# The MLP's first product as seven quadrant products, in two passes over its weights

## The chip, the core and the metric

The kernel runs on one core of a Trainium2 chip. The metric is device microseconds of one execution. Engines: PE (TensorE, matmuls and transposes), DVE (VectorE), ACT (ScalarE), POOL (GpSimd), and SP, whose queue issues nearly all DMAs.

## The reference

Two transformer blocks run one after the other on 1024 tokens of 1024 channels, in float32. The change touches only the last part of the second block, a squared-ReLU MLP with 4096 hidden channels:

```python
def sqrelu_mlp(h, ln_g, w1, w2):
    u = rmsnorm_2(h, ln_g) @ w1          # [1024, 1024] @ [1024, 4096]
    return jnp.square(jax.nn.relu(u)) @ w2   # [1024, 4096] @ [4096, 1024]

def second_block(x, ...):
    h = x
    h = h + hybrid_mixer(h, ...)         # ends in a product with w_out
    h = h + sqrelu_mlp(h, ln_ff_g, w_ff1, w_ff2)
    return rmsnorm_2(h, ln_final_g)
```

## The kernel before

The program is recorded first and then put in order: every engine call goes through `Program.record` (line 346 issues nearly all instructions, so the profile's lines say L346 throughout), each gets a cost from a price table, and `flush` picks on each engine the ready operation of highest priority (the longest chain behind it). The result is a fixed order for each of the five queues; each engine then works through its row in order and waits by semaphores. SBUF is two areas, one for float32 tiles (`sbuf_61` in the order's rows) and one for tiles that PE reads (`sbuf_62`). Addresses are reused: a tile that is laid over a freed one waits for the last use of the old one.

Float32 products are made of three matmuls. Each operand is split into a high half (rounded by an ACT copy) and a low half (DVE: operand minus high half), and `mm3` adds hi x hi, hi x lo and lo x hi in PSUM. One matmul is 128 x 128 x 512.

The part around the change, in program order:

- `mixer2` ends with the out-projection. In two column halves of 512, for each of eight row tiles of 128 tokens, `tok_block` makes 24 matmuls (8 channel blocks x 3), and `ev_o` adds the result on DVE to the residual `xres[tt]`, which is loaded from `hb_d`. A row tile is final after its part in the second column half.
- `mlp` norms each row tile (`normed_T`): the sum of squares on ACT, two small operations on POOL, the scaling on DVE, then eight PE transposes into two PSUM banks, evacuated by ACT (high half) and DVE (low half) into `h`, which overlays `self.y`, the input of the out-projection.
- Then 16 rounds `e` of 256 hidden channels. `chan_block` makes 128 hidden channels for the 1024 tokens: 2 token halves x 8 channel blocks x 3 matmuls, weights as the stationary operand; ACT takes the ReLU and its square (high half), DVE the low half. Then the second product for these 256 hidden channels: 2 column halves x 8 row tiles x 2 x 3 matmuls, each group of six added by DVE to `xres[tt]`. So every row tile is updated in every round and becomes final in the last one.
- Weights come by SP in pieces of 512 KB into a ring `wraw`, and are split into slots `whi`, `wlo`.
- At the end each row tile is normed (ACT, two on POOL, DVE) and stored.

Of the kernel before, what the change touches and what calls it, by code (L numbers as in the profile page):

```python
# [561 lines left out]
class Kern:  # L562
# [1471 lines left out]

    def normed_T(self, pn, x, row, h, tt):
        r = self.sumsq(pn, x, 'nt')
# [263 lines left out]
                                  sr.rearrange("p h e -> p (h e)"))  # L2300


    def mlp(self):
# [4 lines left out]
        with ExitStack() as cn:
            pn = self.pool('pn2', ctx=cn)
            row = self.bcast_row(ins['ln_ff_g_2'][0], D, 'row', pn)  # L2310
            for tt in range(NT):
                self.normed_T(pn, self.xres[tt], row, h, tt)
        for tag in ('whi', 'wlo'):
            self.wp.trim(tag, 3)
        self.nw = 3
        with ExitStack() as cu:
            pu = self.pool('pu', ctx=cu)
            for e in range(16):
                uh, ul = [self.t(pu, [128, 2, T], F32R, tag=n) for n in ('uh', 'ul')]
                for m in range(2):  # L2320
                    def ev_u(half, tok, p):
                        t = self.t(pu, [128, 512], tag='ut', bufs=2)
                        nc.scalar.activation(t, p, AF.Relu)
                        nc.scalar.activation(uh[:, m, tok], t, AF.Square)
                        V.tensor_tensor(out=t, in0=t, in1=t, op=OP.mult)
                        V.tensor_tensor(out=ul[:, m, tok], in0=t, in1=uh[:, m, tok], op=OP.subtract)
                    self.chan_block(w1, 256 * e + 128 * m, 128, h, ev_u)
                for cb in range(2):
                    cs = slice(512 * cb, 512 * cb + 512)
                    wh, wl = self.wload(w2, 256 * e, 512 * cb, 2, 512)  # L2330
                    for tt in range(NT):
                        ts = slice(tt * 128, tt * 128 + 128)
                        p = self.ps([128, 512], 'acc')
                        for k in range(2):
                            self.mm3(p, uh[:, k, ts], ul[:, k, ts], wh[:, k], wl[:, k], k == 0, k == 1)
                        V.tensor_tensor(out=self.xres[tt][:, cs], in0=self.xres[tt][:, cs], in1=p, op=OP.add)
        self.cy.close()
        with ExitStack() as cf:
            pf = self.pool('pf2', ctx=cf)
            row = self.bcast_row(ins['ln_final_g_2'], D, 'row', pf)  # L2340
            for tt in range(NT):
                xt = self.xres[tt]
# [24 lines left out]
```

## Time and profile before

| | |
|---|---|
| median of three runs | 2778.71 us (2775.88 to 2780.1) |
| the profiled execution | 2776.61 us, its span 2774.8 us |
| mean granted TensorE clock | 0.981 |
| busy over the span | PE 94%, DVE 61%, ACT 40%, POOL 22% |
| out-projection's last column half, MLP and end | about 2017 us to 2774.8 us |
| DMA over the span | 468.83 MB, mean 169 GB/s |

A time is given from the start of the span. Busy time of PE counts pipelined matmuls; the granted clock of 1.00 is 2.4 GHz, 0.50 is 1.2 GHz. A row "x3077 | 693.63" means that many instructions in so much busy time; behind a group, the idle time of its engine ahead of it and what ended that.

### The profile page before, as it was taken

Reading aid. Unit: us, or ns where it says so; the run is one execution under the profiler, and the core shown is the slowest. Engines: PE = TensorE matmul, PEld = TensorE weight load, DVE = VectorE, ACT = ScalarE, POOL = GpSimd, SP = SyncE. Lnnn points to the kernel's source line nnn. Section 1 sums busy time; section 2 is a strip of 40 time slices with the busy share of each in tenths; the row PEclk is TensorE's granted clock in tenths of the full one; section 3 lists DMA queues with packets and bytes.
Section 4 is the critical chain, followed back from the end, with each engine's and each line's share of the span. In section 5 each row is a group of like instructions: output and inputs, shape, how many; then the busy total and the mean of one; then the engine's idle time right before and its main releaser. Section 6 shows DMA issues by size and latency. Waiting matters only on the chain. (4 is left out here: it accounts for less than half of the span.)

```text
span 2774.8 us, 35356 instructions
## 1 busy us (share of the span) xinstructions
PE 2609.8 (94%) x12662; PEld 1995.2 (72%) x12662; DVE 1680.3 (61%) x2585; ACT 1104.0 (40%) x1935; POOL 602.2 (22%) x651
## 2 busy tenths in 40 slices
PE   5999999989869999999969999999999999999998
PEld 4787778977657765553526777777888888888886
DVE  8567865556789898676855433377345444444445
ACT  5334332332247676555635432377232212212122
POOL 3016532323431112222234111343100000000001
PEclk9999999999979999999989999999999999999999
DMA  7248586474369999989976423443211111111111
GB/s 248 80 130 239 185 246 178 149 259 153 130 233 352 343 352 333 361 317 359 323 264 218 120 92 105 140 119 82 88 46 47 53 46 54 42 50 54 46 54 68
DMA packets 315792, 468.83 MB, mean 169 GB/s; under 512 B 70170, under 2 KB 140494, under 8 KB 312542
## 3 DMA queue, kind: packets, MB, share of 16 engines
q1 hardware_dynamic: 308958, 449.76, 48.9%
q0 software_dynamic: 6656, 16.79, 1.8%
q8 instruction: 100, 1.64, 0.2%
q14 instruction: 78, 0.64, 0.1%
HBM read 395.62 MB, written 76.76 MB: 170 GB/s over the span
## 5 line engine op out<-in xcount | busy, mean ns | idle before, releaser
L346 PE MATMUL psum_all<-sbuf 128*128 128x512 f32 (+7 forms) x12662 | 2609.8, 367 | 152.5 <-DVE sbuf L346 100.8
L346 PEld LDWEIGHTS psum_all<-sbuf 128*128 128x128 f32 (+4 forms) x12662 | 1995.2, 176 | 766.6 <-issue 159.6
L346 ACT ACTIVATE sbuf<-sbuf 128x1024 fp32r<-128x1024 f32 (+9 forms) x792 | 707.6, 914 | 759.7 <-PE psum_all L346 509.2
L346 DVE TENSOR_TENSOR sbuf<-sbuf,sbuf 128x1024 fp32r<-128x1024 f32 (+3 forms) x538 | 621.1, 1175 | 253.1 <-ACT sbuf L346 246.4
L346 ACT ACTIVATE sbuf<-psum_all 128x512 f32<-128x512 f32 (+14 forms) x774 | 364.2, 481 | 855.8 <-PE psum_all L346 801.1
L346 POOL TENSOR_TENSOR sbuf<-sbuf 128x512 f32<-128x512 f32 (+9 forms) x301 | 361.5, 1209 | 507.6 <-DVE sbuf L346 342.8
L346 DVE TENSOR_TENSOR sbuf<-sbuf 128x512 f32<-128x512 f32 (+16 forms) x345 | 212.0, 628 | 205.3 <-ACT sbuf L346 168.7
L346 DVE TENSOR_TENSOR sbuf<-sbuf,psum_all 128x512 f32<-128x512 f32 (+3 forms) x327 | 217.3, 672 | 161.4 <-PE psum_all L346 161.1
L346 POOL TENSOR_SCALAR sbuf<-sbuf 128x1 f32<-128x1 f32 (+3 forms) x182 | 77.5, 427 | 1031.4 <-ACT sbuf L346 928.7
L346 DVE TENSOR_TENSOR sbuf<-psum_all,sbuf 128x512 f32<-128x512 f32 (+12 forms) x306 | 182.1, 607 | 161.3 <-ACT sbuf L346 82.3
L346 DVE SCALAR_TENSOR_TENSOR sbuf<-sbuf 128x512 f32<-128x512 f32 (+5 forms) x247 | 198.6, 810 | 46.8 <-POOL sbuf L346 36.4
L346 DVE TENSOR_SCALAR sbuf<-sbuf 128x32 f32<-128x32 f32 (+7 forms) x220 | 109.3, 509 | 62.2 <-ACT sbuf L346 42.9
L1808 POOL DMA_INDIRECT y_d<-sbuf x35 | 57.4, 1641 | 195.6 <-DVE sbuf L346 194.4
L346 DVE SCALAR_TENSOR_TENSOR sbuf<-sbuf,psum_all 128x128 f32<-128x128 f32 (+1 forms) x100 | 38.2, 410 | 86.7 <-PE psum_all L346 55.9
L1796 POOL DMA_INDIRECT sbuf<-h_d,sbuf x35 | 44.6, 1273 | 187.0 <-PE psum_all L346 154.0
L346 DVE SCALAR_TENSOR_TENSOR sbuf<-psum_all,sbuf 128x128 f32<-128x128 f32 (+9 forms) x109 | 62.0, 586 | 38.1 <-PE psum_all L346 37.6
L346 DVE CUSTOM_DVE_ANT_0 sbuf<-psum_all,sbuf 128x512 f32<-128x512 f32 (+2 forms) x80 | 48.1, 613 | 23.3 <-PE psum_all L346 22.7
L346 POOL MEMSET sbuf<- 64x64 f32 (+10 forms) x54 | 16.9, 313 | 194.7 <-DVE sbuf L346 114.1
L346 POOL TENSOR_TENSOR sbuf<-sbuf,sbuf 128x1024 fp32r<-128x1024 f32 x16 | 41.1, 2570 | 40.2 <-ACT sbuf L346 39.5
L346 ACT ACTIVATE sbuf<-psum_all,sbuf 128x128 f32<-128x128 f32 (+1 forms) x72 | 24.4, 403 | 35.4 <-PE psum_all L346 22.9
L346 ACT ACTIVATION_READ_ACCUMULATOR sbuf<-sbuf 128x1 f32 x152 | 28.9, 190 | 0.0
L346 DVE COPY sbuf<-psum_all 128x512 f32<-128x512 f32 (+9 forms) x31 | 15.1, 488 | 22.2 <-PE psum_all L346 18.8
(18 smaller groups left out, 112.2 us busy)
## 6 DMA issues: line engine op xcount, KB each, us to landing
sbuf<-in_w SPq DMA_DIRECT2D x384, 512.0 KB
sbuf<-in_w_ff SPq DMA_DIRECT2D x64, 512.0 KB
sbuf<-in_w_in SPq DMA_DIRECT2D x56, 512.0 KB
sbuf<-in_w_ada SPq DMA_DIRECT2D x48, 512.0 KB
sbuf<-in_x SPq DMA_DIRECT2D x16, 512.0 KB
sbuf<-qkv_d SPq DMA_DIRECT2D x32, 256.0 KB
pre_d<-sbuf SPq DMA_DIRECT2D x8, 1024.0 KB
sbuf<-pre_d SPq DMA_DIRECT2D x8, 1024.0 KB
```

The costliest lines, as they stand in the source:

```text
L346: op = self.new_op(eng, lambda: real(*a, **k), name, reads, writes)
L1796: return self.prog.real.gpsimd.indirect_dma_start(out=xg, out_offset=None, in_=self.h2_d, in_offset=bass.IndirectOffsetOnAxis(ap=tok, axis=0),
L1808: st = self.prog.real.gpsimd.indirect_dma_start(out=self.y_d, out_offset=bass.IndirectOffsetOnAxis(ap=dest, axis=0), in_=y, in_offset=None ...
```

## The change

The product u = n @ w1 is made transposed, as w1^T n^T, and cut in 2 x 2 quadrants: A by 512 hidden and 512 input channels within a column group of 1024 hidden channels (four groups `g`), B (`b11`, `b21`, `b12`, `b22`) by 512 input channels and 512 tokens. Winograd's form of Strassen's algorithm makes the four quadrants of u from seven products of quadrants, P1 to P7, in place of eight:

- P1 = A11 B11, P2 = A12 B21, P7 = (A11 - A21) x b7, P6 = S2 x b6 with S2 = A22 - A11 + A21, P5 = (A11 + S2) x b5, P3 = (A12 - S2) x b3, P4 = A22 x b4; b3 is B22 itself, and b4 to b7 are sums and differences of the B quadrants.

Pass 1 makes P1, P2, P7 and P6 for all four groups. P1 + P2 is a quadrant of u and is stored to `u_d`; P1 + P6 and P1 + P6 + P7 are stored to `k_d`, and S2 to `s_d`. Pass 2 loads these and weights again and makes P5, P3 and P4, with the other three quadrants of u stored to `u_d`. Four split B quadrants fit on chip at a time. Then the second product loads u back in units of 256 hidden channels, squares and splits it, and accumulates 512 hidden channels in PSUM (12 matmuls) before DVE adds to the residual. The residual goes to `x_d` and back. Token halves are the outer loop of the second product within 512 hidden channels. The pool of mixer 2 (`c0`) is released ahead of the out-projection instead of behind it.

```diff
@@ mixer2
+        c0.close()
         self.banks = {'acc': (0, 1, 2, 3), 'tp': (4, 5), 'sm': (6, 7)}
...
         for tt in range(NT):
             self.tap('hm', self.xres[tt], slice(tt * 128, tt * 128 + 128))
-        c0.close()
@@ new helpers
+    def halved(self, x, hi=None, lo=None):
...
+        nc.scalar.activation(hi, x, AF.Copy)
+        nc.vector.tensor_tensor(out=lo, in0=x, in1=hi, op=OP.subtract)
+        return hi, lo
+    def quad_product(self, n, A, B, evac):
+        ops = [self.halved(a) for a in A]
+        self.nprod += 1
+        ps = [self.prog.psum_tile([128, 512], 'quad', (4 * (self.nprod % 2) + t,)) for t in range(4)]
+        first = None
+        for j, (ah, al) in enumerate(ops):
+            for t, p in enumerate(ps):
+                m = slice(128 * t, 128 * t + 128)
+                for k in range(2):
+                    bh, bl = [b[:, 2 * j + k] for b in B]
+                    for i, (x, y) in enumerate(((ah, bh), (ah, bl), (al, bh))):
+                        op = nc.tensor.matmul(p, x[:, k, m], y, start=j + k + i == 0, stop=j + k + i == 4)
+                        first = first or op
+                        op.head = first
+        for t, p in enumerate(ps):
+            evac(n, t, p)
@@ mlp, the norm
+                V.scalar_tensor_tensor(t, x, r, row, op0=OP.mult, op1=OP.mult)
+                for k in range(2):
+                    p = self.ps([128, 4, 128], 'tp')
+                    for i in range(4):
+                        nc.tensor.transpose(p[:, i, :], t[:, 512 * k + 128 * i:512 * k + 128 * i + 128], self.ident)
+                    b = q[f'b{k + 1}{tt // 4 + 1}'][:, :, 128 * (tt % 4):128 * (tt % 4) + 128]
+                    if k:
+                        V.tensor_copy(b, p)
+                    else:
+                        nc.scalar.activation(b, p, AF.Copy)
+                nc.sync.dma_start(x_d[tt * 128:tt * 128 + 128], x)
@@ mlp, pass 1
+        b1, b2 = bsplit('b11', 0), bsplit('b21', 1)
+        both(V, 'b12', 'b22', 'b12', OP.subtract)
+        b7 = bsplit('b12', 2)
+        both(V, 'b12', 'b11', 'b12', OP.add)
+        b6 = bsplit('b12', 3)
+        both(G, 'b11', 'b22', 'b12', OP.subtract)
+        both(G, 'b21', 'b21', 'b12', OP.subtract)
+        for g in range(4):
+            a11, a12, a21, a22 = wq(g, 0, 0), wq(g, 0, 1), wq(g, 1, 0), wq(g, 1, 1)
+            def ev(n, t, p):
+                u, v = keep[0][t], keep[1][t]
+                if n in (1, 7):
+                    nc.scalar.activation(u if n == 1 else v, p, AF.Copy)
+                elif n == 2:
+                    out(g, 0, 0, t, u, p)
+                else:
+                    V.tensor_tensor(out=u, in0=u, in1=p, op=OP.add)
+                    V.tensor_tensor(out=v, in0=u, in1=v, op=OP.add)
+                    for i, x in enumerate((u, v)):
+                        nc.sync.dma_start(k_d[128 * g:128 * g + 128, 2048 * i + 512 * t:2048 * i + 512 * t + 512], x)
+            self.quad_product(1, a11, b1, ev)
+            for x, y in zip(a11, a21):
+                V.tensor_tensor(out=y, in0=x, in1=y, op=OP.subtract)
+            self.quad_product(2, a12, b2, ev)
+            self.quad_product(7, a21, b7, ev)
+            for j, (x, y) in enumerate(zip(a22, a21)):
+                V.tensor_tensor(out=y, in0=x, in1=y, op=OP.subtract)
+                nc.sync.dma_start(s_d[128 * g:128 * g + 128, 1024 * j:1024 * j + 1024], y.rearrange("p a n -> p (a n)"))
+            self.quad_product(6, a21, b6, ev)
@@ mlp, pass 2
+        b5, b3, b4 = bsplit('b11', 0), bsplit('b22', 1), bsplit('b21', 2)
+        for g in range(4):
...
+            for t in range(4):
+                for i in range(2):
+                    nc.sync.dma_start(keep[i][t], k_d[128 * g:128 * g + 128,
+                                                      2048 * i + 512 * t:2048 * i + 512 * t + 512])
+            def ev(n, t, p):
+                u, v = keep[0][t], keep[1][t]
+                if n == 5:
+                    out(g, 1, 1, t, v, p)
+                    V.tensor_tensor(out=u, in0=u, in1=p, op=OP.add)
+                elif n == 3:
+                    out(g, 0, 1, t, u, p)
+                else:
+                    out(g, 1, 0, t, v, p)
...
+            self.quad_product(5, a11, b5, ev)
...
+            self.quad_product(3, a12, b3, ev)
+            self.quad_product(4, a22, b4, ev)
@@ mlp, second product
+        for g in range(8):
+            def act(j, th):
+                a = self.t(pa, [128, 2, 512], tag='u', bufs=6)
+                r = ((2 * g + j) * 2 + th) * 128
+                nc.sync.dma_start(a, u_d[r:r + 128].rearrange("p (a n) -> p a n", a=2))
+                V.scalar_tensor_tensor(a, a, 0.0, a, op0=OP.max, op1=OP.mult)
+                return self.halved(a)
+            for th in range(2):
+                A = [act(j, th) for j in range(2)]
+                for cb in range(2):
...
+                        for j in range(2):
+                            for k in range(2):
+                                (ah, al), (wh, wl) = A[j], W[cb][j]
+                                self.mm3(p, ah[:, k, m], al[:, k, m], wh[:, k], wl[:, k], j + k == 0, j + k == 2)
+                        x = xres[4 * th + t][:, cs_]
+                        V.tensor_tensor(out=x, in0=x, in1=p, op=OP.add)
```

`out` adds two tiles on DVE and stores the sum to `u_d`; `bsplit` is `halved` of a B quadrant in two halves; `both` is one operation on a B quadrant in two halves of 128x1024, on DVE (`V`) or POOL (`G`); `wq` loads a weight quadrant in two pieces of 512 KB.

The instructions' order, at three places. First PE's row from the last row tiles of the out-projection on. A MATMUL of 128x128 is a transpose here, one of 128x512 belongs to a product. Before:

```order
L346 MATMUL psum_all<-sbuf_62 128x512 x24
L346 MATMUL psum_all<-sbuf_61 128x128 x8
L346 MATMUL psum_all<-sbuf_62 128x512 x24
L346 MATMUL psum_all<-sbuf_61 128x128 x8
L346 MATMUL psum_all<-sbuf_62 128x512 x24
L346 MATMUL psum_all<-sbuf_61 128x128 x8
L346 MATMUL psum_all<-sbuf_62 128x512 x2
L346 MATMUL psum_all<-sbuf_61 128x128 x8
L346 MATMUL psum_all<-sbuf_62 128x512 x10
L346 MATMUL psum_all<-sbuf_61 128x128 x4
L346 MATMUL psum_all<-sbuf_62 128x512 x6
L346 MATMUL psum_all<-sbuf_61 128x128 x4
```

After, from the same place:

```order
L347 MATMUL psum_all<-sbuf_62 128x512 x156
L347 MATMUL psum_all<-sbuf_61 128x128
L347 MATMUL psum_all<-sbuf_62 128x512 x24
L347 MATMUL psum_all<-sbuf_61 128x128 x7
L347 MATMUL psum_all<-sbuf_62 128x512 x5
L347 MATMUL psum_all<-sbuf_61 128x128
L347 MATMUL psum_all<-sbuf_62 128x512 x19
L347 MATMUL psum_all<-sbuf_61 128x128 x31
L347 MATMUL psum_all<-sbuf_62 128x512 x6
L347 MATMUL psum_all<-sbuf_61 128x128 x24
L347 MATMUL psum_all<-sbuf_62 128x512 x2874
```

The transposes stood in eights between products; now 55 of the 64 stand in two blocks with six product matmuls between (four of P1, two of P2), ahead of the other 2874.

Second, DVE's row at the same place, from the adds of row tiles 2 to 6 on (COPY evacuates four transposes, SCALAR_TENSOR_TENSOR norms a row tile, a `sbuf_62` result is a low half). Before, where these adds stand apart:

```order
L346 TENSOR_TENSOR sbuf_61<-sbuf_61,psum_all 128x512
L346 SCALAR_TENSOR_TENSOR sbuf_61<-sbuf_61 128x1024
L346 TENSOR_TENSOR sbuf_61<-sbuf_61,psum_all 128x512 x3
L346 TENSOR_TENSOR sbuf_62<-psum_all,sbuf_62 128x4x128
L346 TENSOR_TENSOR sbuf_61<-sbuf_61,psum_all 128x512
L346 SCALAR_TENSOR_TENSOR sbuf_61<-sbuf_61 128x1024
L346 TENSOR_TENSOR sbuf_62<-psum_all,sbuf_62 128x512
L346 TENSOR_TENSOR sbuf_62<-psum_all,sbuf_62 128x4x128
L346 TENSOR_TENSOR sbuf_61<-sbuf_61,psum_all 128x512
L346 SCALAR_TENSOR_TENSOR sbuf_61<-sbuf_61 128x1024
L346 TENSOR_TENSOR sbuf_62<-psum_all,sbuf_62 128x512
L346 TENSOR_TENSOR sbuf_62<-psum_all,sbuf_62 128x4x128
```

After:

```order
L347 TENSOR_TENSOR sbuf_61<-sbuf_61,psum_all 128x512 x5
L347 COPY sbuf_61<-psum_all 128x4x128
L347 SCALAR_TENSOR_TENSOR sbuf_61<-sbuf_61 128x1024
L347 TENSOR_TENSOR sbuf_62<-sbuf_61,sbuf_62 128x1024 x3
L347 COPY sbuf_61<-psum_all 128x4x128
L347 SCALAR_TENSOR_TENSOR sbuf_61<-sbuf_61 128x1024
L347 COPY sbuf_61<-psum_all 128x4x128
L347 SCALAR_TENSOR_TENSOR sbuf_61<-sbuf_61 128x1024
L347 COPY sbuf_61<-psum_all 128x4x128
L347 SCALAR_TENSOR_TENSOR sbuf_61<-sbuf_61 128x1024
L347 TENSOR_TENSOR sbuf_61<-sbuf_61,psum_all 128x512
L347 COPY sbuf_61<-psum_all 128x4x128
```

The low half of the transposed tile, a 128x512 subtraction from PSUM, is now a copy, and the normalisations and copies have moved behind the add of row tile 6.

Third, SP's row where pass 1 goes over into pass 2 (before, this queue held only `in_w_ff` loads here):

```order
L347 DMA sbuf_61<-in_w_ff_2 128x2x512
L347 DMA sbuf_61<-k_d 128x512
L347 DMA k_d<-sbuf_61 128x512
L347 DMA sbuf_61<-k_d 128x512
L347 DMA sbuf_61<-x_d 128x1024
L347 DMA sbuf_61<-k_d 128x512
L347 DMA sbuf_61<-in_w_ff_2 128x2x512
L347 DMA sbuf_61<-k_d 128x512
L347 DMA sbuf_61<-s_d 128x1024
L347 DMA u_d<-sbuf_61 128x512
L347 DMA sbuf_61<-k_d 128x512
L347 DMA sbuf_61<-in_w_ff_2 128x2x512
```

Loads of kept sums from `k_d` stand behind their stores, with weight loads, `s_d` and `x_d` loads and the `u_d` stores of P5 between.

## Rows read from the trace of the kernel before

**Rows 1.** The cores' view: span and mean granted clock.

```profile
core 0: 2774.8 us, clock 0.981
```

**Rows 2.** Groups by shape, 2000 to 2775 us: count, busy, mean ns, idle.

```profile
L346 PE MATMUL psum_all<-sbuf 128*128 128x128 f32 x68 | 9.7, 274 | 0.1
L346 DVE TENSOR_TENSOR sbuf<-sbuf,psum_all 128x512 f32<-128x512 f32 x267 | 179.9, 683 | 110.1 <-PE psum_all L346 110.1
L346 DVE TENSOR_TENSOR sbuf<-sbuf,sbuf 128x1024 fp32r<-128x1024 f32 x67 | 82.0, 1223 | 145.1 <-ACT sbuf L346 144.8
L346 ACT ACTIVATE sbuf<-sbuf 128x1024 fp32r<-128x1024 f32 x67 | 71.1, 1061 | 371.6 <-PE psum_all L346 371.0
L346 ACT ACTIVATE sbuf<-psum_all 128x512 f32<-128x512 f32 x64 | 37.6, 588 | 174.0 <-PE psum_all L346 173.9
L346 DVE SCALAR_TENSOR_TENSOR sbuf<-sbuf 128x1024 f32<-128x1024 f32 x16 | 20.4, 1282 | 6.5 <-POOL sbuf L346 5.6 <-PE psum_all L346 0.6
```

**Rows 3.** MLP stretch: sum, busy (count) PE, PEld, DVE, ACT, POOL; clock; DMA.

```profile
2061.89:2755.52 693.63, 693.63 (x3077) 574.46 (x3078) 329.74 (x455) 146.74 (x204) 2.06 (x6) 1.00 0.15 47
```

**Rows 4.** Waits of PE, 2000 to 2775 us: total us, times, longest.

```profile
PE psum_all L346 <- ACT sbuf L346: 1.2, 1, 1.2
```

**Rows 5.** PE in order of time, hand-over: start us, us; in brackets idle before.

```profile
2016.81 43.02 PE L346 MATMUL psum_all<-sbuf 128*128 128x512 f32 x203
2061.07 44.12 PE L346 MATMUL psum_all<-sbuf 128*128 128x512 f32 x209 [1.25 <-ACT sbuf L346]
```

**Rows 6.** PE in order of time and stretches of 2 us around 1815 us.

```profile
1815.74 8.45 PE L346 MATMUL psum_all<-sbuf 128*128 128x288 f32 x40 [2.15 <-DVE sbuf L346]
...
1816.00:1818.00 2.00, 2.00 (x9) 1.98 (x10) 2.00 (x9) 0.91 (x3) 0.57 (x2) 0.50 0.79 255
1818.00:1820.00 2.00, 2.00 (x8) 1.50 (x7) 1.15 (x4) 1.31 (x3) 0.81 (x3) 0.50 0.28 68
1820.00:1822.00 2.00, 2.00 (x12) 1.72 (x12) 1.16 (x5) 1.35 (x3) 1.60 (x2) 0.75 0.31 70
```

**Rows 7.** The end: instructions in order of time; in brackets idle before.

```profile
2755.54 0.69 DVE L346 TENSOR_TENSOR sbuf<-sbuf,psum_all 128x512 f32<-128x512 f32 x1 [0.24 <-PE psum_all L346]
...
2756.32 1.06 ACT L346 ACTIVATE sbuf<-sbuf 128x1024 bf16<-128x1024 f32 x1 [1.55 <-DVE sbuf L346]
...
2757.83 0.55 POOL L346 TENSOR_TENSOR sbuf<-sbuf 128x1 f32<-128x1 f32 x1
...
2758.86 1.28 DVE L346 SCALAR_TENSOR_TENSOR sbuf<-sbuf 128x1024 f32<-128x1024 f32 x1
...
2768.18 1.29 DVE L346 SCALAR_TENSOR_TENSOR sbuf<-sbuf 128x1024 f32<-128x1024 f32 x1 [0.72 <-POOL sbuf L346]
```

**Rows 8.** Stretches by DMA share and GB/s (last two columns), and an array's transfers.

```profile
258.00:260.00 2.00, 2.00 (x10) 1.65 (x9) 2.00 (x5) 0.00 (x0) 0.74 (x1) 1.00 0.99 161
...
860.00:900.00 40.00, 39.57 (x186) 30.41 (x185) 37.09 (x40) 29.68 (x36) 6.01 (x4) 1.00 0.98 365
...
1440.00:1450.00 10.00, 2.46 (x10) 2.07 (x10) 7.46 (x8) 5.82 (x9) 6.03 (x9) 0.50 1.01 415
...
L346 SPq DMA_DIRECT2D hb_d<-sbuf x8: 319/320/1146, 1446.4 to 1495.8; - x8
```

**Rows 9.** Waits of SP's queue, whole span: total us, times, longest.

```profile
SPq L346 <- DMA x_d<-sbuf: 11.0, 3, 4.0
```

**Rows 10.** Copy and POOL groups; then DVE and POOL at 255 us.

```profile
L346 POOL TENSOR_TENSOR sbuf<-sbuf,sbuf 128x1024 fp32r<-128x1024 f32 x16 | 41.1, 2570 | 40.2 <-ACT sbuf L346 39.5
...
L346 DVE COPY sbuf<-psum_all 128x512 f32<-128x512 f32 (+9 forms) x31 | 15.1, 488 | 22.2 <-PE psum_all L346 18.8
...
254.94 1.49 POOL L346 TENSOR_TENSOR sbuf<-sbuf 128x512 f32<-128x512 f32 x1
...
255.45 1.26 DVE L346 TENSOR_TENSOR sbuf<-sbuf 128x256 f32<-128x256 f32 x1
...
261.01 0.41 DVE L346 TENSOR_TENSOR sbuf<-sbuf 128x256 f32<-128x256 f32 x1
```

More of the change, by code (lines that the diff above doesn't have):

```diff
@@ L49 @@
 RMW = ('copy_predicated',)
+SLOTS = (4, 6), (5, 7), (0, 1), (2, 3)
 class Op:
@@ L2300, in gla @@
                                   sr.rearrange("p h e -> p (h e)"))
+    def halved(self, x, hi=None, lo=None):
+        nc = self.nc
+        if hi is None:
+            hi, lo = [self.t(self.wp, [128, 2, 512], F32R, tag=n, bufs=self.nw) for n in ('whi', 'wlo')]
+        nc.scalar.activation(hi, x, AF.Copy)
+        nc.vector.tensor_tensor(out=lo, in0=x, in1=hi, op=OP.subtract)
+        return hi, lo
+    def quad_product(self, n, A, B, evac):
+        nc = self.nc
+        ops = [self.halved(a) for a in A]
[13 more added lines that the diff above has]
+            evac(n, t, p)
     def mlp(self):
         nc, ins = self.nc, self.ins
-        V = nc.vector
+        V, G = nc.vector, nc.gpsimd
         w1, w2 = ins['w_ff1_2'][0], ins['w_ff2_2'][0]
-        h = self.y
+        self.nprod = 1
+        x_d = self.dt([T, D], 'x_d')
+        u_d = self.dt([32 * 128, 1024], 'u_d')
+        k_d = self.dt([4 * 128, 4096], 'k_d')
+        s_d = self.dt([4 * 128, 2048], 's_d')
+        cq, cw = ExitStack(), ExitStack()
+        pq = self.pool('qb', ctx=cq)
+        pw = self.pool('pw', ctx=cw)
+        q = {n: self.t(pq, [128, 4, 512], tag=n) for n in ('b11', 'b21', 'b12', 'b22')}
+        pw.reserve('wraw', 1024, 2)
         with ExitStack() as cn:
@@ L2311, in mlp @@
             for tt in range(NT):
-                self.normed_T(pn, self.xres[tt], row, h, tt)
-        for tag in ('whi', 'wlo'):
[L2314 to L2327, printed above, removed]
-                for cb in range(2):
[L2329 to L2336, printed above, removed]
@@ new lines, in mlp @@
+                nc.sync.dma_start(x_d[tt * 128:tt * 128 + 128], x)
+        self.cxp.close()
+        self.cy.close()
+        cs = ExitStack()
+        pb = self.pool('bs', ctx=cs)
+        tiles = [self.t(pb, [128, 4, 512], F32R, tag=f'b{i}') for i in range(8)]
+        slots = [(tiles[i], tiles[j]) for i, j in SLOTS]
+        cu = ExitStack()
+        pu = self.pool('pu', ctx=cu)
+        keep = [[self.t(pu, [128, 512], tag=f'k{i}{t}') for t in range(4)] for i in range(2)]
+        pw.reserve('wraw', 1024, 5)
@@ new lines, in mlp, with bsplit, both @@
+        self.raws, self.nunit, self.nw = [(self.wp, 3), (pw, 7)], 0, 5
+        def bsplit(name, n):
+            hi, lo = slots[n]
+            for j in range(2):
+                s = slice(2 * j, 2 * j + 2)
+                self.halved(q[name][:, s], hi[:, s], lo[:, s])
+            return hi, lo
+        def both(eng, out, a, b, op):
+            for j in range(2):
+                s = slice(2 * j, 2 * j + 2)
+                eng.tensor_tensor(out=q[out][:, s], in0=q[a][:, s], in1=q[b][:, s], op=op)
@@ new lines, in wq, with out @@
+        def wq(g, i, k):
+            c = 1024 * g + 512 * i
+            return [self.wraw(w1[512 * k + 256 * j:512 * k + 256 * j + 256, c:c + 512].rearrange(
+                "(a p) n -> p a n", p=128), 2, 512) for j in range(2)]
+        def out(g, i, j, t, a, b):
+            u = self.t(pu, [128, 512], tag='u', bufs=4)
+            V.tensor_tensor(out=u, in0=a, in1=b, op=OP.add)
+            c = 8 * g + 4 * i + t
+            r = (c // 2 * 2 + j) * 128
+            nc.sync.dma_start(u_d[r:r + 128, 512 * (c % 2):512 * (c % 2) + 512], u)
@@ new lines, in mlp @@
+        cu.close()
+        cq.close()
+        cs.close()
+        self.cxp = ExitStack()
+        xp = self.pool('x3', ctx=self.cxp)
+        xres = [self.t(xp, [128, D], tag=f'x{tt}') for tt in range(NT)]
+        for tt in range(NT):
+            nc.sync.dma_start(xres[tt], x_d[tt * 128:(tt + 1) * 128])
+        pa = self.pool('ua', ctx=cw)
+        pa.reserve('u', 1024, 6)
+        for tag in ('whi', 'wlo'):
+            self.wp.reserve(tag, 1024, 8, F32R)
+        self.nw = 13
+        for g in range(8):
[5 more added lines that the diff above has]
+                return self.halved(a)
+            W = {}
+            for th in range(2):
+                A = [act(j, th) for j in range(2)]
+                for cb in range(2):
+                    if not th:
+                        W[cb] = [self.wload(w2, 512 * g + 256 * j, 512 * cb, 2, 512) for j in range(2)]
+                    cs_ = slice(512 * cb, 512 * cb + 512)
+                    for t in range(4):
+                        p = self.prog.psum_tile([128, 512], 'y', tuple(range(8)))
+                        m = slice(128 * t, 128 * t + 128)
+                        for j in range(2):
+                            for k in range(2):
[3 more added lines that the diff above has]
+                        V.tensor_tensor(out=x, in0=x, in1=p, op=OP.add)
@@ L2338, in mlp @@
+        cw.close()
         with ExitStack() as cf:
@@ L2341, in mlp @@
             for tt in range(NT):
[L2342 removed]
+                xt = xres[tt]
                 r = self.sumsq(pf, xt, 'fn')
```

11 lines of the change are left out of this document (10 added, 1 removed).

## The prediction

> **What bounds the kernel now.** I read the span first [rows 1], then the MLP stage, which is all that the change touches: the groups by shape [rows 2], the stretches [rows 3], the waits [rows 4] and TensorE's order of time [rows 5]. From 2061.89 to 2755.52 us PE is busy for every one of 693.63 us at granted clock 1.00; it holds 3077 matmuls, so one 128x128x512 matmul costs 693.63 / 3077 = 0.2255 us [rows 3]. In the whole stage from 2000 us on PE waits once, for 1.2 us [rows 4]; DVE is busy 0.48 of the time and ACT 0.21 [rows 3]. So the stage is a count of matmuls at 0.2255 us, and the only other things in it that set the end are the hand-over from the out-projection (1.25 us idle at 2061.07 [rows 5]) and the end, 19.3 us from the last matmul (2755.52) to the end of the span [rows 7].
>
> **The change part by part.** All sums are made against the profiled execution: 2776.61 us, span 2774.8, 1.8 outside it; the median of the runs is 2.1 above it.
>
> *Matmuls.* Before, the first product has 32 blocks x 2 halves x 8 k x 3 = 1536, the second 1536. After, the first is 4 column groups x 7 products x 48 = 1344; the second stays 1536. 192 x 0.2255 = **-43.3 us**, all on the path. The Trainium skill, TensorE: Matmul & The Clock Gate, section "Wait — 56ns, not 53.3ns?", gives 215.7 ns for 512 columns; by it the term would be -41.4. The row decides.
>
> *Hand-over from the out-projection.* Let E be the end of its last matmul. Before, PE's row has the norm's transposes in eights between out-projection matmuls. After, 55 of the 64 stand behind E, and all of them ahead of the first product save six matmuls. They need DVE's results: per row tile a normalisation (1.28) and a PSUM copy (0.49). On DVE's row behind E stand the rest of a weight split, 5 normalisations, 6 copies, the last add and the first low half of b11 before P1 can go on: 1.35 + 5 x 1.28 + 6 x 0.49 + 0.68 + 1.22 = 12.6 us [rows 2, 10], plus the square-and-POOL chain of the last tile that DVE waits for and the two transpose banks, about 1.6 (estimate from [rows 7]): P1 runs from E + 14.3. PE's own work in this time is 55 x 0.143 (9.7 / 68, [rows 2]) + 6 x 0.2255 = 9.2. Idle 5.1 against 1.25 before: **+3.9 us**; bounds 0 (the waits overlap better) and +10 (DVE's row runs later by one more tile chain of 4.6).
>
> *TensorE's clock there.* Before 1815.74 us PE was idle for 2.15 us, after which the granted clock was 0.50 for two slices of 2 us and 0.75 in a third, so about 5 us at 1.2 GHz where it had 2.4 [rows 6]; that costs about half of it. The hand-over has more idle than that stretch, in pieces of about 1 us. I take **+3.0**; bounds 0 and +6.
>
> *Splits, sums and evacuations.* Pass 1, per column group (192 matmuls, 43.3 us): DVE 12 of 1.22 and 12 of 0.68 = 22.9; ACT 8 x 1.06 + 8 x 0.59 = 13.2. Pass 2, per group (144 matmuls, 32.5 us): DVE 10 x 1.22 + 16 x 0.68 = 23.1, ACT 6.4. Second product, per 512 channels (43.3 us): DVE 4 x (1.28 + 1.22) + 4 x 1.22 + 16 x 0.68 = 25.8 [rows 2]. All lie beside PE's work at 53, 71 and 60%: nothing on the path, as long as operands are made ahead. Five slots of split weights, two for a product, give one and a half products (16 us) of lead. If that cover goes, each us of DVE lateness is a us.
>
> *POOL's subtractions.* Four of 2.57 [rows 10] for the second pass's quadrants. At 255 us a DVE 128x256 operation that takes 0.41 alone took 1.26 beside a POOL operation [rows 10]; at that price the four hold DVE up for 4 x 0.85 = 3.4. They fall beside P2, P7 and P6 of the first group, where DVE's row ends its work for P6 some 5 us before P6 begins (estimate: the 12.6 of above, 9 more of 1.22 and 8 of 0.68 behind it, against four products of 10.8): nothing on the path. The Trainium skill, SBUF — State Buffer, section "SBUF: two separate sides", has a rule against this: a DVE operation with two SBUF inputs and a GpSimd one that reads SBUF lock each other out for whole instructions. By it the four would hold DVE up for as much as 10.3, and the term would be up to +5.
>
> *Transfers.* Pass 1, per group: 8 weight loads and 2 s_d stores of 512 KB, 8 k_d and 4 u_d stores of 256 KB, 8.4 MB in 43.3 us = 194 GB/s; pass 2: 8 loads of 512 KB, 8 k_d loads and 12 u_d stores of 256 KB, 9.4 MB in 32.5 us = 290 GB/s. Where 512 KB loads alone run the core moved 365 GB/s, and 415 where x_d loads and hb_d stores mix [rows 8]. So there is room on average. SP issues in order, and a u_d store there waits for DVE with weight and k_d loads queued behind it. The tightest place is between the passes: 16 k_d transfers, four weight and s_d loads and an x_d load, some 6.5 MB, for stores that start about 2 us before the last product of pass 1 ends. At 365 GB/s that is 18 us; DVE needs the k_d tiles to free the banks of P5 before P4, 21.6 us later. A load waited up to 4.0 us for a store to the same array [rows 9]. I take **+2.0** for this and all such waits; bounds 0 and +15.
>
> *Start of the second product.* Its first weights overwrite the split quadrant that P4 reads to its last matmul: ACT 1.06 and the hand-over, 1.3, and 0.4 behind the next split: **+1.7**; bounds 0 and +4.
>
> *End.* Before, all eight row tiles become final within the last 11 us, and ACT, POOL and DVE need until 2769.47. After, four are final 21.6 us earlier and the others 24 matmuls (5.4 us) apart, so only the last chain is left: add at 2755.54 to end of the normalisation at 2760.14, 4.6, and output store to end, 2774.8 - 2769.47 = 5.3 [rows 7]: 9.9 instead of 19.3, **-9.4**; bounds -6 and -11.
>
> *At nothing:* the earlier release of the pool of mixer 2 (c0.close) moves addresses only: no instruction goes with it. The x_d round trip of the residual: its stores wait on SP for each row tile and weight loads stand behind them, but P7 and P6, which use these, come 20 us later.
>
> Sum: -43.3 + 3.9 + 3.0 + 2.0 + 1.7 - 9.4 = -42.1; 2776.6 - 42.1 = 2734.5, and with the 2.1 to the median **2736 us**.
>
> **The rivals.**
> *Transfers become the bound (slower).* At 258 to 260 us the sixteen queues were 0.99 busy with 161 GB/s [rows 8]. If the mix of stores and loads in the two passes ran at that, 4 x (8.4 + 9.4) = 71 MB would take 443 us where PE needs 303: +140, 2876 us. It decides from 207 GB/s, where the passes take 345 us and the gain of 42 is gone. Against it: rows of 2 KB and more on both sides, as in the 365 GB/s stretch, while that stretch has mixer 1's small pieces. Chance 0.07.
> *Operands late.* DVE at 71% in pass 2, in order, held at its P5 sums by k_d loads; each held product makes PE wait. At 2 us for each of the 12 products of pass 2: +24, 2760 us. For it: three engines and one queue in fixed order, and DVE at 0.48 on average in this stage before. Against it: the lead of 16 us, and P3's and P4's splits stand ahead of the first k_d wait on DVE's row. Chance 0.2.
> *The hand-over costs nothing.* No clock fall, idle as before: -6.9 more, 2729 us. Chance 0.12.
> *The matmuls aren't saved.* TensorE's row behind the transposes holds 2874 matmuls and six before, 2880 instead of 3072; excluded.
>
> **How the numbers follow.** The forecast, 2730 to 2746, has 0.57; late operands 0.2 (2746 to 2770), the free hand-over 0.12 (2723 to 2730), transfers as bound 0.07, other losses 0.04. From 2724 to 2757: 0.57, most of 0.12 and half of 0.2, about 0.8. A measurement of this kernel can tell about 0.2%, 5.6 us. Faster: 0.57 + 0.12 + 0.2 and a little of the rest = 0.91; same 0.02; slower 0.07.
>
> **What would show it.** In the profile after: 2880 matmuls of 128x512 behind the transposes at 0.2255 us each; PE idle of about 5 us in pieces around the last transposes with a granted clock below 1.00 in a slice behind them; PE at full share through pass 1, pass 2 and the second product, with GB/s near 190, 290 and 95; about 10 us from last matmul to end. Wrong would be: waits of PE for DVE in pass 2, DMA share near 1 there, SP waiting on k_d stores for long, or a hand-over beyond 20 us.

## The result, and the profile after

The changed kernel takes 2735.7 us (median of six, 2730.92 to 2739.58) beside 2777.29 us (2774.66 to 2780.1): a ratio of 0.985, 95% interval 0.9837 to 0.9862. That is 41.6 us less; the forecast was 2736. The total was met; the terms for the end, the clock and the waits in the passes were not, and they cancelled, as the trace shows.

The profiled execution took 2739.58 us, its span is 2737.8, the longest of the six; [rows 1] has 2774.8. The two profiles already differ ahead of the stage: the same work there ends 4.5 us later in the one of after. So I counted off the stage by instructions of PE, from the end backwards: 3072 or 2880 matmuls of the MLP, its 64 transposes, and the same 356 instructions ahead of them, which is the last 3492 of before and the last 3300 of after. The stretches are rows of the stretches' view (start to the end of the span; length, busy time and count of PE, PEld, DVE, ACT, POOL; granted clock, DMA share, GB/s). Before, then after:

```profile
1980.10:2774.80 794.70, 780.87 (x3492) 645.87 (x3490) 370.59 (x502) 174.34 (x248) 21.01 (x36) 0.99 0.16 51
```

```profile
1984.61:2737.80 753.19, 739.00 (x3300) 609.88 (x3298) 437.63 (x488) 184.65 (x214) 37.23 (x40) 1.00 0.46 159
```

The stage is 794.70 - 753.19 = 41.5 us shorter with 192 matmuls fewer. A second profile of the same kernel, below, has 753.22 for it: the runs' spread of 5 to 10 us lies ahead of the stage, and inside it tenths of a us can be read.

PE's order of time in after, from the out-projection on (start, us, engine, line, operation, count; in brackets the idle time before and who ended it), answers to [rows 5]:

```profile
1999.72 63.31 PE L347 MATMUL psum_all<-sbuf 128*128 128x512 f32 x290
2063.90 1.09 PE L347 MATMUL psum_all<-sbuf 128*128 128x128 f32 x8 [0.87 <-ACT sbuf L347]
2065.68 1.09 PE L347 MATMUL psum_all<-sbuf 128*128 128x128 f32 x8 [0.69 <-DVE sbuf L347]
2067.46 3.68 PE L347 MATMUL psum_all<-sbuf 128*128 128x128 f32 x22 [0.69 <-DVE sbuf L347]
2071.68 1.42 PE L347 MATMUL psum_all<-sbuf 128*128 128x128 f32 x8 [0.55 <-DVE sbuf L347]
2073.85 304.73 PE L347 MATMUL psum_all<-sbuf 128*128 128x128 f32 x1346 [0.74 <-DVE sbuf L347]
2379.49 348.73 PE L347 MATMUL psum_all<-sbuf 128*128 128x512 f32 x1536 [0.92 <-ACT sbuf L347]
```

Five pieces of idle around the blocks of transposes (3.5 us together), then both passes without a single wait (2073.85 to 2378.58), 0.92 us of idle, and the second product, 1536 matmuls without a wait. The passes and the second product as stretches answer to [rows 3]:

```profile
2379.49:2728.22 348.73, 348.73 (x1536) 288.13 (x1536) 186.96 (x216) 64.15 (x69) 5.17 (x14) 1.00 0.24 82
2075.00:2246.00 171.00, 171.00 (x754) 141.60 (x755) 118.49 (x118) 59.17 (x71) 20.23 (x4) 1.00 0.66 220
2246.00:2378.00 132.00, 132.00 (x584) 109.27 (x584) 91.08 (x109) 31.19 (x31) 0.00 (x0) 1.00 0.87 308
```

The clock is 1.00 throughout, DVE is busy 0.69 in each pass (118.49 / 171.00, 91.08 / 132.00), and the transfers run at 220 and 308 GB/s. The chain of waits says 303.38 us of PE for the passes and 318.07 for most of the second product; it names no DMA.

**The end.** It is 2728.22 to 2737.8, 9.6 us, as forecast. But in the kernel before it had not been the 19.3 that the forecast compared it with. This is the stretch of before that the forecast took for the time behind the last matmul [rows 7]:

```profile
2755.52:2774.80 19.28, 6.78 (x30) 5.26 (x29) 12.43 (x13) 6.91 (x12) 8.61 (x13) 0.78 0.54 218
```

PE still works on 30 matmuls in it; the row of PE that holds them, by time:

```profile
2749.67 12.63 PE L346 MATMUL psum_all<-sbuf 128*128 128x512 f32 x55
```

Its last matmul ends at 2762.30, 12.5 us ahead of the end. So the new end is worth about 12.5 - 9.6 = 2.9 us, not 9.4.

### The profile page after: what moved, and what is told of

Read it like the earlier page. It is cut to its first block, busy times and chain, and to the rows that moved or that the text cites. A ratio compares the mean times of both kernels' runs of the same rounds, so it can differ in the third digit from the quotient of the medians.

```text
span 2737.8 us, 35489 instructions
## 1 busy us (share of the span) xinstructions
PE 2574.1 (94%) x12470; PEld 1964.1 (72%) x12470; DVE 1746.6 (64%) x2571; ACT 1114.5 (41%) x1901; POOL 616.7 (23%) x655
## 4 chain that ended last, share of the span: by engine, by line
PE 44%; issue 2%; DVE 1%; DMA 1%; POOL 1%; ACT 1%; POOLq 0%; SPq 0%; DVEq 0%; ACTq 0%
PE psum_all L347 44%; DVE sbuf L347 1%; POOL sbuf L347 1%; ACT sbuf L347 1%; DMA sbuf<-in_w 0%; DMA y_d<-sbuf 0%; DMA qk_d<-sbuf 0%; DMA sbuf<-in_w_out 0%; DMA sbuf<-y_d 0%; DMA sbuf<-gla_d 0%; DMA sbuf<-in_k_l 0%; POOLq L2522 0%; POOLq L347 0%; POOLq L1734 0%; SPq L617 0%
## 5 line engine op out<-in xcount | busy, mean ns | idle before, releaser
L347 PE MATMUL psum_all<-sbuf 128*128 128x512 f32 (+11 forms) x12470 | 2574.1, 367 | 154.1 <-DVE sbuf L347 103.1
L347 PEld LDWEIGHTS psum_all<-sbuf 128*128 128x128 f32 (+7 forms) x12470 | 1964.1, 176 | 763.7 <-issue 159.4
L347 ACT ACTIVATE sbuf<-sbuf 128x1024 fp32r<-128x1024 f32 (+9 forms) x798 | 739.6, 949 | 878.9 <-PE psum_all L347 443.7
L347 DVE TENSOR_TENSOR sbuf<-sbuf,sbuf 128x1024 fp32r<-128x1024 f32 (+3 forms) x544 | 664.7, 1245 | 190.0 <-ACT sbuf L347 181.4
L347 ACT ACTIVATE sbuf<-psum_all 128x512 f32<-128x512 f32 (+12 forms) x734 | 341.4, 476 | 690.8 <-PE psum_all L347 638.5
L347 POOL TENSOR_TENSOR sbuf<-sbuf 128x512 f32<-128x512 f32 (+9 forms) x305 | 379.6, 1253 | 530.2 <-DVE sbuf L347 363.2
L347 DVE TENSOR_TENSOR sbuf<-sbuf,psum_all 128x512 f32<-128x512 f32 (+3 forms) x295 | 196.0, 671 | 225.0 <-PE psum_all L347 221.3
L347 DVE TENSOR_TENSOR sbuf<-sbuf 128x256 f32<-128x256 f32 (+16 forms) x333 | 224.2, 691 | 87.0 <-ACT sbuf L347 31.6
L347 DVE SCALAR_TENSOR_TENSOR sbuf<-sbuf 128x1024 f32<-128x1024 f32 (+5 forms) x279 | 237.4, 857 | 60.5 <-POOL sbuf L347 37.7
L347 DVE TENSOR_TENSOR sbuf<-psum_all,sbuf 128x512 f32<-128x512 f32 (+12 forms) x290 | 171.4, 603 | 160.3 <-ACT sbuf L347 73.2
```

What stands on the lines that cost most here:

```text
L347: op = self.new_op(eng, lambda: real(*a, **k), name, reads, writes)
```

## The experiments

Two accounts of the 41.5 us were to be told apart. **The trace's account:** 192 x 0.2266 = 43.5 for the matmuls (the row below, a stretch of before with matmuls alone, holds 2900 in 657.0 us, which is 0.2266 each), 2.9 for the end, and 4.9 lost at the hand-over and at the second product's start; nothing for the clock or for waits in the passes. **The forecast's account:** 43.3 and 9.4 gained, 10.6 lost in four places. Each run's stage is the row of its last 3300 (or 3492) instructions of PE, as above.

```profile
2098.50:2755.50 657.00, 657.00 (x2900) 544.04 (x2899) 306.04 (x423) 133.76 (x183) 1.30 (x4) 1.00 0.15 46
```

**Seven of eight channel blocks.** The kernel before, the first product summed over 896 of 1024 input channels, so that 192 matmuls are missing (the other users of `chan_block` keep `nk` = 8).

```diff
-            for k in range(8):
+            for k in range(nk):
...
-                    self.chan_block(w1, 256 * e + 128 * m, 128, h, ev_u)
+                    self.chan_block(w1, 256 * e + 128 * m, 128, h, ev_u, 7)
```

> The kernel before, with the eighth of the eight channel blocks left out of the MLP's first product: 192 matmuls of 128x512 fewer, and nothing else changed (its output is that of the shorter product). Theory 1 (the stage is a count of matmuls): a matmul takes 0.2267 us in both traces, so 192 x 0.2267 = 43.5 us less, about 2734, with TensorE's row as full as before. Theory 2 (the gain of 41.5 came partly from elsewhere in the new second product and end, and the matmuls are worth less, since DVE and ACT have to keep up with a shorter product): 30 to 38 us less, and waits of PE for ACT or DVE in the stage.

Measured: 2734.5 us, ratio 0.984 (0.9819 to 0.9861). The stage:

```profile
1981.00:2732.20 751.20, 737.35 (x3300) 609.83 (x3298) 370.56 (x502) 174.39 (x248) 21.02 (x36) 0.99 0.17 54
```

794.70 - 751.20 = 43.5 us, to the tenth; PE waits once for 1.2 us, as in before. Theory 1: the matmul term is the whole of the gain, and everything else that the change does comes out at about +2.

**The end alone.** The kernel before with the last of the 16 rounds in another order.

```diff
-                for cb in range(2):
+                w = [self.wload(w2, 256 * e, 512 * cb, 2, 512) for cb in range(2)]
+                for cb, tt in ([(c, t) for c in range(2) for t in range(NT)] if e < 15 else
+                               [(c, t) for t in range(NT) for c in range(2)]):
...
-                    for tt in range(NT):
```

The weights of both column halves are now loaded ahead of the loop in every round. In the last round a row tile becomes final every 12 matmuls here; in the changed kernel's trace the last ones are 5.4 us apart, which is 24 matmuls and not 12.

> The kernel before with the last round's second product made row tile by row tile (both column halves of a row tile behind each other), so that row tiles become final 12 matmuls apart as in the changed kernel, instead of 6. Theory 1 (TensorE of before ended near 2762.1, 12.7 us ahead of the end, and not at 2755.52): from the last matmul to the end about 9.7 us, so 3 us less, 2774. Theory 2 (the forecast's term): 9.4 us less, 2768.

Measured: 2774.33 us, ratio 0.9991 (0.9982 to 1.0001), which by itself could be nothing; the stage can tell it:

```profile
1980.33:2772.10 791.77, 780.87 (x3492) 645.87 (x3490) 370.22 (x502) 174.34 (x248) 18.06 (x36) 1.00 0.16 51
```

2.9 us, and PE's 780.87 us are those of before. Theory 1. Where the 2.9 come from is seen in the last two row tiles. Before (two operations on POOL, of one element per partition, and the normalisation on DVE):

```profile
2764.67 1.47 POOL L346 TENSOR_TENSOR sbuf<-sbuf 128x1 f32<-128x1 f32 x1
...
2766.17 1.28 DVE L346 SCALAR_TENSOR_TENSOR sbuf<-sbuf 128x1024 f32<-128x1024 f32 x1 [0.44 <-POOL sbuf L346]
2766.22 1.28 POOL L346 TENSOR_SCALAR sbuf<-sbuf 128x1 f32<-128x1 f32 x1
2767.59 0.55 POOL L346 TENSOR_TENSOR sbuf<-sbuf 128x1 f32<-128x1 f32 x1
```

and with the row tiles further apart:

```profile
2764.60 0.19 POOL L346 TENSOR_SCALAR sbuf<-sbuf 128x1 f32<-128x1 f32 x1 [1.90 <-ACT sbuf L346]
2764.88 0.55 POOL L346 TENSOR_TENSOR sbuf<-sbuf 128x1 f32<-128x1 f32 x1
2765.46 1.28 DVE L346 SCALAR_TENSOR_TENSOR sbuf<-sbuf 128x1024 f32<-128x1024 f32 x1 [1.01 <-POOL sbuf L346]
```

The same small operation takes 1.28 us where a normalisation runs beside it and 0.19 where DVE is idle; beside an add with an operand in PSUM (2759.17 in this run) it takes 0.19 too. In before four normalisations still stood in DVE's queue behind the last matmul (2762.30).

**The end put back.** The changed kernel, its last unit of 512 hidden channels in the order of before.

```diff
+            if g == 7:
...
+                for j in range(2):
+                    for cb in range(2):
+                        for tt in range(NT):
...
+                            for k in range(2):
+                                self.mm3(p, ah[:, k, m], al[:, k, m], wh[:, k], wl[:, k], k == 0, k == 1)
```

> The changed kernel with the last unit of the second product in the order of before: six matmuls and an add for each of the eight row tiles in turn, so that all row tiles become final in the last 11 us. Theory 1 (the new end is worth 2.9 us): last matmul to end 12.7 instead of 9.7, 2739. Theory 2 (the forecast's term of 9.4): 2745.

Measured: 2739.47 us, ratio 0.9852 (0.9836 to 0.9869); the stage:

```profile
1982.82:2736.40 753.58, 739.00 (x3300) 609.79 (x3298) 449.02 (x504) 184.66 (x214) 37.49 (x40) 1.00 0.47 160
```

Only 0.4 more, which neither theory expected. The run doesn't tell them apart, because the planner did not bring the row tiles as close together as the written order has them. The last five row tiles' squares on ACT start at 2716.65, 2720.75, 2722.97, 2725.68 and 2727.48, so they are 1.8 to 4.1 us apart, where those of before are 1.2 to 2.0 apart (2758.16 to 2764.09).

**The norm first.** The changed kernel, the norm's operations with a higher priority in the planner.

```diff
+            self.prog.boost = 90000.0
             for tt in range(NT):
                 x = self.xres[tt]
...
+                self.prog.boost = 0.0
                 nc.sync.dma_start(x_d[tt * 128:tt * 128 + 128], x)
+                self.prog.boost = 90000.0
+            self.prog.boost = 0.0
```

> The changed kernel with a higher priority in the planner for the norm ahead of the MLP: its transposes go in eights between products again, 22 matmuls of the first product stand ahead of the last eight. Theory 1 (the hand-over costs the 3.5 us in which PE waits for DVE's row): PE idle there falls from 3.5 to about 1 us, 2.5 less, 2733. Theory 2 (the waits only move: P1 then waits for the split of the b11 quadrant instead): idle stays at 3 to 5 us, 2736 to 2738.

Measured: 2733.78 us, ratio 0.9839 (0.982 to 0.9857). The stage, and PE's order of time from the hand-over on:

```profile
1985.78:2733.80 748.02, 737.43 (x3300) 609.80 (x3298) 438.30 (x488) 184.38 (x214) 34.19 (x40) 1.00 0.47 161
```

```profile
2039.71 334.84 PE L347 MATMUL psum_all<-sbuf 128*128 128x512 f32 x1499
2375.48 24.82 PE L347 MATMUL psum_all<-sbuf 128*128 128x512 f32 x107 [0.92 <-ACT sbuf L347]
```

The hand-over has no idle left, so the price was the order, not the amount of work on DVE: theory 1, and by more than it said. The gain in the stage, 753.19 - 748.02 = 5.2 us, is the 3.5 of idle and 1.6 of PE's busy time (739.00 against 737.43). About half of the latter is seen in the changed kernel's hand-over, where nine product matmuls between 2062 and 2075 us take 2.8 us and not 2.0; why was not taken apart. The kernel before had 1.25 us of idle at this place, so against it the hand-over of the changed kernel costs 5.2 - 1.25 = 3.9 us.

**The norm slower.** The changed kernel, each normalisation made three times.

```diff
-                V.scalar_tensor_tensor(t, x, r, row, op0=OP.mult, op1=OP.mult)
+                for _ in range(3):
+                    V.scalar_tensor_tensor(t, x, r, row, op0=OP.mult, op1=OP.mult)
```

> The changed kernel with each normalisation of the norm ahead of the MLP made three times by DVE (same result), 2.56 us more on DVE per row tile. Theory 1 (DVE's row sets the hand-over, and pieces of idle do not lower the granted clock): about four row tiles lie behind the out-projection's last matmul, so 10 us more idle of PE in longer pieces, clock 1.00, about 2746. Theory 2 (the clock falls as soon as the pieces reach 2 us, as at 1815 us before): the same idle and a stretch at 0.50 behind it, 3 us more, about 2749.

Measured: 2748.17 us in one run. The stage, then stretches of the hand-over:

```profile
1982.38:2746.40 764.02, 743.30 (x3300) 613.48 (x3298) 456.90 (x504) 185.02 (x214) 40.47 (x40) 0.99 0.46 157
```

```profile
2062.00:2066.00 4.00, 1.91 (x12) 1.53 (x12) 4.00 (x5) 3.97 (x7) 1.06 (x1) 1.00 0.69 251
2066.00:2070.00 4.00, 1.50 (x6) 0.72 (x4) 4.00 (x5) 0.62 (x2) 1.45 (x1) 0.66 0.14 20
2070.00:2074.00 4.00, 3.89 (x14) 2.88 (x14) 3.12 (x4) 2.66 (x4) 0.00 (x0) 0.50 0.64 221
...
2078.00:2080.00 2.00, 0.76 (x4) 0.79 (x5) 2.00 (x3) 0.00 (x0) 0.00 (x0) 0.50 0.00 0
2080.00:2082.00 2.00, 2.00 (x11) 1.53 (x9) 1.67 (x3) 0.60 (x1) 0.00 (x0) 0.50 0.79 239
```

10.8 us more in the stage, and a clock at 1.2 GHz (from 2074 to 2078, where PE is nearly idle, the granted clock is 0.96 and 0.89). PE's idle pieces are 0.78, 1.70, 1.93, 0.68 and 5.11 us here, 10.2 in all, 6.7 more than in the changed kernel, where both theories had 10; the other 4.1 lie in busy time, part of it at the low clock (not separated further). Theory 2 as to the clock: it can be a cost of the hand-over. Here it fell behind pieces of 1.70 and 1.93 us; with five pieces of 0.55 to 0.87 us, in the changed kernel, it stayed at 2.4 GHz.

**More traffic.** Each load of a kept sum made twice.

```diff
-                    nc.sync.dma_start(keep[i][t], k_d[...])
+                    for _ in range(2):
+                        nc.sync.dma_start(keep[i][t], k_d[...])
```

> The changed kernel with each load of a kept sum from k_d in pass 2 made twice: 8 loads of 256 KB more per column group, 8.4 MB in all. Theory 1 (pass 2 has just room: 308 GB/s at a DMA share of 0.87, so some 355 GB/s at full share; 46 MB then take 130 us, as long as PE needs): 0 to 5 us more, about 2738. Theory 2 (the transfers are already on the edge, since stretches stand at 0.95): the 8.4 MB come on top, 24 us, about 2760, with PE waiting.

Measured: 2746.81 us in one run (its work ahead of the stage 1.8 us later than in the changed kernel's profile). The stage, a stretch of 132 us around pass 2 (its last matmul ends at 2381.76), and two slices at the second product's start:

```profile
1986.41:2744.80 758.39, 741.11 (x3300) 610.97 (x3298) 436.40 (x488) 184.43 (x214) 37.30 (x40) 0.99 0.49 169
```

```profile
2256.00:2388.00 132.00, 128.02 (x558) 104.87 (x557) 84.97 (x102) 29.86 (x30) 0.00 (x0) 0.99 0.97 350
...
2386.00:2388.00 2.00, 1.95 (x5) 1.62 (x6) 2.00 (x3) 0.01 (x1) 0.00 (x0) 0.60 0.95 280
2388.00:2390.00 2.00, 2.00 (x6) 1.53 (x5) 2.00 (x3) 0.00 (x0) 0.00 (x0) 0.55 1.03 349
```

5.2 us for 8.4 MB: just beyond theory 1's 0 to 5, and far from 24. Pass 2 had some 40 GB/s of room; at 350 GB/s and a share of 0.97 PE begins to wait, 1.12 us in the last column group of pass 2 and 2.86 in three pieces (1.46, 0.82, 0.58) around the second product's start. That is 3.1 us more idle than in the changed kernel. The other 2.1 are busy time (741.11 against 739.00), and the two slices show where most of it lies: behind those three pieces the granted clock was 0.60 and 0.55.

**Fewer slots.** Three slots of split weights in the passes.

```diff
-        self.raws, self.nunit, self.nw = [(self.wp, 3), (pw, 7)], 0, 5
+        for tag in ('whi', 'wlo'):
+            self.wp.trim(tag, 3)
+        self.raws, self.nunit, self.nw = [(self.wp, 3), (pw, 7)], 0, 3
...
-            self.wp.reserve(tag, 1024, 8, F32R)
+            self.wp.reserve(tag, 1024, 10, F32R)
```

The last line keeps the second product at 13 slots, as in the changed kernel.

> The changed kernel with three instead of five slots of split weights in the two passes: operands are ready at most half a product ahead (5.4 us) instead of one and a half (16 us). Theory 1 (the three engines need only a few us of lead; a slot takes 1.06 + 1.22 us to fill): 0 to 5 us more, about 2738. Theory 2 (the lead of 16 us is what hides DVE's row in pass 2): about 2 us of waiting for each of the 28 products, 2790.

Measured: 2735.15 us in one run; the stage:

```profile
1981.00:2733.20 752.20, 738.87 (x3300) 609.97 (x3298) 438.71 (x488) 184.66 (x214) 30.31 (x40) 1.00 0.47 160
```

1.0 us less than with five, and behind the first column group (from 2114.47 on) PE has no wait at all, not even at the second product's start. The likely reason, which no row shows, is that with other slots in turn its first weights no longer lie on the quadrant that P4 reads. Theory 1, and more than it: in this run the lead of 16 us is not needed.

**The subtractions on DVE.**

```diff
-        both(G, 'b11', 'b22', 'b12', OP.subtract)
-        both(G, 'b21', 'b21', 'b12', OP.subtract)
+        both(V, 'b11', 'b22', 'b12', OP.subtract)
+        both(V, 'b21', 'b21', 'b12', OP.subtract)
```

> The changed kernel with the four subtractions of POOL (second pass's quadrants) made by DVE. In the changed kernel the first took POOL 11.2 us, and three DVE subtractions beside the others took 3.0 to 3.4 us instead of 1.22. Theory 1 (they hold each other up, at no cost to PE): DVE has 4 x 1.22 more of its own and no long ones, PE no wait, time as the changed kernel, 2736. Theory 2 (DVE's row has no room there): PE waits up to 4.9 us for P6's operands, 2740.

Measured: 2740.24 us in one run, of which the stage is that of the changed kernel:

```profile
1985.24:2738.40 753.16, 739.01 (x3300) 610.16 (x3298) 436.15 (x492) 184.78 (x214) 16.98 (x36) 1.00 0.47 160
```

Theory 1. DVE's busy time in the stage is even 1.5 us less, with four operations more (last section).

**Both mends together**, beside the changed kernel again and a version with the last normalisation and store in halves. All three on one chip, with the same runs of the kernel before (2778.03 us).

> The changed kernel unchanged, on the same chip and beside the same runs of the kernel before as the two that follow, 2736.

> The changed kernel with both edits that took waiting away: the norm's higher priority and three slots of split weights in the two passes (with which the second product's first weights no longer wait for the last product of pass 2). Theory 1 (the two places are independent): 5.2 + 1.0 us less than the changed kernel, 2730. Theory 2 (with transposes between products, three slots are too few at the hand-over or behind it): 1 to 4 us less, 2732 to 2735, with waits of PE in the first column group.

> As the run with both edits, and the last normalisation and store of each row tile made in two column halves. Theory 1 (the last store of 512 KB takes 5.3 us from issue to the end, half of it fixed): the first half is stored while the second is normed, 1 to 2 us less, 2728.5. Theory 2 (the store's time is nearly all fixed and DVE has one operation more): 0 to 0.6 us less, 2730.

Measured: the changed kernel 2737.59 us, ratio 0.9853 (0.9837 to 0.9869); both mends 2728.07, ratio 0.9815 (0.98 to 0.983); the halves 2729.72, ratio 0.9833 (0.9817 to 0.9849). The stages, in this order:

```profile
1978.08:2731.30 753.22, 739.02 (x3300) 610.08 (x3298) 437.68 (x488) 184.68 (x214) 37.33 (x40) 1.00 0.47 159
```

```profile
1983.34:2729.80 746.46, 736.85 (x3300) 609.88 (x3298) 438.45 (x488) 184.76 (x214) 35.26 (x40) 1.00 0.47 161
```

```profile
1979.83:2726.30 746.47, 736.87 (x3300) 609.88 (x3298) 439.83 (x496) 184.74 (x214) 35.28 (x40) 1.00 0.47 161
```

With both mends PE has no wait from the out-projection to its last matmul, and the stage is 6.8 us shorter than the changed kernel's: theory 1 (5.2 + 1.0), and 0.6 more. This version beats both kernels. The halves bring nothing (0.0): the last normalisation ends 5.2 us ahead of the end with a last store of 256 KB, 5.3 with one of 512 KB, so halving that store hardly shortened the end: theory 2. What the rest of the 5.2 us goes to is not shown.

## Why the prediction was right, point by point

| term | forecast | measured | from |
|---|---|---|---|
| matmuls | -43.3 | -43.5 | seven of eight blocks |
| hand-over | +3.9 | +3.9: idle 2.3 more, busy 1.6 more | the norm first: 5.2, less the 1.25 of before |
| clock there | +3.0 | 0 | granted clock 1.00 |
| k_d round trip and other waits | +2.0 | 0 | no wait of PE in the passes |
| second product's start | +1.7 | +0.9 to +1.6 | row of idle 0.92; fewer slots 1.0; both mends beside the norm first 1.6 |
| end | -9.4 | -2.9 | the end alone |
| sum | -42.1 | -41.5 | the stage; with 0.9 for the start the terms add up to -41.6 |

- **Matmuls:** right, and for the reason given. The price of 0.2255 (693.63 / 3077 is 0.2254) was an average over a stretch that held some 128x128 transposes, which are shorter, and lacked the last 30 matmuls; a matmul alone is 0.2266. That [rows 3] counted 3077, close to the 3072 that I looked for, hid this.
- **End: the step that failed.** It read 2755.52 as the end of PE's last matmul, because the chain of waits leaves PE there. The chain goes on through the operations that ended last, and a step from PE to DVE or POOL only says that this row tile's sum was ready then; PE had 7 us of work left. The bounds of -6 and -11 came from the same reading and did not hold -2.9. The new end itself (9.9 forecast, 9.6 measured) was right, being read from operations.
- **Clock and waits:** taken at +5.0 and worth nothing. The lower bounds of 0 held both. The clock term came from [rows 6], where an idle of 2.15 us preceded the fall; the pieces here are 0.55 to 0.87 us, near the forecast's own "pieces of about 1 us", and the clock stayed at 1.00. It did fall where the pieces were longer: 1.70 and 1.93 us in the norm slowed down, 1.46 with two shorter ones in more traffic.
- So 6.5 us too much gain at the end and 5 us too much loss in the clock and the waits made a total that is right to the us. That the matmuls bound the stage was right; the accuracy of 2736 (2734.5 + 2.1 is 2736.6) was luck, and the range of 2724 to 2757 was what the argument could carry.
- **Hand-over:** right in place, and its size was met in part by luck: PE was idle for 3.5 us in five pieces (5.1 forecast), and 1.6 us of longer busy time, which the forecast did not have, made up for it. The first product's steady run starts at 2074.98, 13 us behind the out-projection's last matmul (14.3 forecast).
- **POOL:** nothing on the path, as forecast, with DVE held up by 6.2 us where I took 3.4 (last section).
- **Rivals:** transfers as the bound decide from where the mix of loads and stores saturates; 161 GB/s was the wrong row for that, since 350 were reached. The passes moved 220 and 308 GB/s where 194 and 290 were forecast; the transfers between the passes, put at some 6.5 MB, add up to 6.8, or 18.7 us in place of 18, still inside the 21.6. Late operands did not come about even with half the lead: DVE's share of 0.69 in pass 2 was near the 0.71 forecast, and three slots sufficed. In pass 1 it was 0.69 too, where 0.53 was forecast: that sum left out the splits and sums of the B quadrants and the first work for pass 2 (72 operations of 128x1024 from 2075 to 2246 us where it has 48), and PE had room for them all the same. The free hand-over did not come by itself, but a priority in the planner makes it.

## What to carry to other kernels

The end of an engine's work is read from that engine's own order of time, not from the step at which the chain of waits leaves it. Count a stage off by the instructions of its bounding engine: the same kernel gave 753.19 and 753.22 us in two profiles, where the total spread over 9 us, so that a gain of 1 to 3 us could be named. When a change makes a product wait for the steps that prepare its inputs, look at the priority of these steps first: the same operations in another order took the whole hand-over away.
